# A hybrid SSD and MLA layer on one core: TensorE's issue order up to the first FFN tiles is replaced by another

## The chip, the core and the metric

The kernel runs on one core of a Trainium2 chip. The metric is the device time of one execution in microseconds. Three runs of the kernel before gave 641.02, 641.30 and 641.71 us, a median of 641.3 us. One further execution was profiled.

## What is computed

One layer of a streaming encoder in float32, for 512 new tokens of one stream and 64 tokens of another that has a cache of 256. SSD heads and latent attention heads run side by side on one projection; a SwiGLU FFN follows.

```python
h = rmsnorm(x, p['norm_mix'])
proj = h @ p['w_in']                       # z, x/B/C, dt, query latent, key/value latent
xbc, conv_new = causal_conv(xbc, conv_buf, p['conv_w'], p['conv_b'])
y, h_new = ssd_scan(xh, dt, A, Bm, Cm, ssm_h0)
y = y + d_skip * xh
y_ssd = rmsnorm(y * silu(z), p['ssd_norm'])
...
o_lat = mla_attend(q_lat, q_rope, q_pos, keys_c, keys_r, jnp.arange(P + T))
o = einsum('bthl,lhd->bthd', o_lat, w_uv)
x = x + concatenate([y_ssd, o], -1) @ p['w_out']
hf = rmsnorm(x, p['norm_ffn'])
x = x + (silu(hf @ p['w_gate']) * (hf @ p['w_up'])) @ p['w_down']
```

The model is 1024 wide, the FFN 2816; there are 8 SSD heads of 64 channels with 128 states, and 8 attention heads of 64. Outputs are the final norm of x, the new latents, the SSD states and the last convolution rows.

## The kernel before

All 576 tokens lie along the free dimension and channels along the 128 partitions. TensorE (PE) works with two kinds of products.

- Weight products are split in two float32r parts each and summed over three products: `product` (L120 to L130, the input projection), `product_halves` (L435 to L446, the gate z, the query and key tiles ps_q and ps_k, the output projection ps_o), `v_tiles` (ps_v, L590) and `block_product` (L852, the FFN). A tile of tokens is 288 columns, half of 576.
- Products of data with data stay float32, and each is recorded as two passes: the SSD's ps_y, ps_i and ps_s (L527, L538, L548), the sums ps_g (L572), the scores sc and sc_s (L657, L663), and the values pv and pvs (L704, L715). Transposes through the identity (ps_x, ps_b, ptp; L483, L491, L679, L687) are float32 too, with one pass each.

Some of the float32 products use only half of PE's columns. ps_y has 64 channels for each head: the even head writes partitions 0 to 63 and the odd head 64 to 127, as two products of 64 columns that stand one behind the other in the program. sc_s (the scores of the 64 late tokens), pv and pvs are built in the same way. The profile shows the columns in the shape: `128*64` or `100*64` or `64*64` where the others read `128*128`. With one exception (ps_v of the 64-token block) the float32r products are 128 columns wide.

In the order of the program: eight steps that load x and the first weights (ps_first), the twelve tiles of the input projection with convolution (ps_in, then ps_z), five SSD chunks (`chunk_a`, `chunk_e`, `chunk_b`, `chunk_s`, `gate`, numbered 4, 0, 1, 2, 3; chunk 4 is the 64-token stream), four pairs of attention heads (`scores`, `soft`, `turn`, `values`), the output projection, and the FFN. The FFN's first tile is ps_p (`gu_first`); from the second on the tiles are called ps_x, ps_y and ps_z again, and the down projection ps_d.

PSUM holds three buffers called sc, three pp and two hm. VectorE (DVE) takes the row maximum of each score tile (mx, L640), ScalarE (ACT) the exponential (pr, L641), which is the last reader of an sc buffer. The reader of ps_y on DVE is L532.

Each engine's order is written out by hand in the table `ISSUE`, by numbers of the instructions in the order in which the code makes them. `issue_in_order` at the end of the kernel ties each instruction to the one ahead of it, so an engine executes in exactly that order, and every engine waits in its place for what it needs:

```python
order = list(_places(text))
for a, b in zip(order, order[1:]):
    tc.add_manual_dep(made[b], made[a].name, info, reason="issue order")
```

Of the kernel before, what the change touches and what calls it, by code (L numbers as in the profile page):

```python
# [1295 lines left out]
def issue_in_order(tc, nc):  # L1296
# [10 lines left out]

ISSUE = {
    "PE": """
0-7 20-21 8 14-16 9-13 22-25 38-41 17-19 32-36 26-31 42-43 56-59 37 50-55 68-69 44-47 60-61 74-79 92 48-49 62-67 80-85  # L1310
98-99 93-97 70-73 86-91 104-106 100-103 110 107-109 122-126 134-135 111-115 128-133 148-153 116-121 136-141 127
142-147 154-169 174-175 170-171 270-274 176-221 172-173 222-269 275-370 373-420 371 421-468 372 469-634 637 641-644
638-640 657-660 635-636 665-697 661 698-718 662 737-758 719-720 663-664 721-726 763 645-652 759-760 727-736 764-766
653-656 767-768 771-794 769-770 795-818 859 761-762 819-826 860-861 833-836 862-864 837-840 827-832 865-870 841-845
871-872 846-852 873-874 853-856 875-877 880 878-879 857-858 881-887 904-911 888 912 892-899 889-891 900-903 925-926
913-921 927-935 922-924 939-940 936-938 949-957 964-966 941 945-948 967 958-963 968-969 942-944 970-975 987 976-979
1003 980-986 991-993 988 1004-1005 1015-1021 1006-1014 1022-1024 994-996 1025-1026 1029-1034 1043-1045 997-998 989
1000-1002 999 1046-1054 990 1035-1039 1059-1061 1040-1042 1062-1064 1027-1028 1075-1077 1081-1092 1055-1056 1078-1080
1057 1093-1096 1058 1097-1104 1121-1123 1071-1072 1124-1129 1065 1068-1070 1073 1105-1107 1066-1067 1074 1130-1143
1119 1144-1156 1120 1229-1232 1157 1108-1112 1233-1240 1113-1114 1158 1241-1245 1115-1118 1159-1161 1246-1247 1176  # L1320
1253-1262 1177 1248-1252 1263-1264 1162-1175 1180 1178 1181-1182 1265 1183 1266-1268 1277-1278 1179 1279 1184-1187
1190-1195 1269-1275 1196-1204 1188-1189 1205-1223 1276 1227-1228 1224-1226 1280-1297 1301-1303 1298-1300 1304-1321
1342-1343 1348-1355 1344-1347 1322-1341 1356-1511 1572 1512-1559 1575-1576 1560-1571 1577 1596-1598 1578 1573-1574
1593 1584-1585 1579 1581-1583 1602-1604 1623-1625 1594-1595 1614 1586 1605-1606 1590-1592 1611-1613 1632-1634
1587-1589 1608-1610 1607 1580 1599-1601 1620-1622 1641 1626-1628 1647-1648 1629-1631 1649 1642-1643 1615-1616
1635-1637 1617-1619 1638-1640 1653 1656 1658-1667 1644-1646 1650-1652 1654-1655 1668-1669 1657 1682 1694-1705
1683-1693 1670-1681 1730-1741 1706-1729 1742-1748 1754-1755 1749-1753 1756-1767 1778-1785 1768-1777 1786-1885
1898-1905 1886-1897 1906-2017 2030-2036 2018-2029 2037-2053 2066-2084 2054-2065 2085-2089 2102-2104 2090-2101
2105-2221 2234-2236 2240-2241 2222-2233 2237 2242-2248 2238-2239 2249-2725 2738-2740 2744 2726-2737 2741 2745-2751
2742-2743 2752-3229 3242-3244 3248 3230-3241 3245 3249-3255 3246-3247 3256-3733 3746-3748 3752 3734-3745 3749  # L1330
3753-3759 3750-3751 3760-4189
""",
    "DVE": """
1 0 2-3 48 4-5 7 6 9 12 8 10-11 13-15 17 16 18-20 23 21-22 49 24 58 25 30 26 85 27-29 31-34 67-68 106 36 69 108 37 105
# [161 lines left out]
```

## Time and profile before

| what | value |
|---|---|
| median of three runs | 641.3 us |
| the profiled execution's own time | 639.76 us |
| its span, first to last instruction | 638.1 us |
| mean granted PE clock | 0.998 |
| PE busy | 627.0 us (98%), 4635 matmul records |
| DVE busy | 543.5 us (85%) |
| ACT busy | 400.9 us (63%) |

A record's start is measured, its end is modelled, and products overlap: a float32r product of 288 columns is listed with some 0.295 us, but the next one starts earlier than that. So the work of PE is read here from one start to the next. In a timeline row the first number is the start, the second the time to the end of the last record of the row, then come the engine, the line, the operation, its output and inputs, the shape and the number of records. A float32 product counts as two records, a transpose as one.

### The profile page before, as it was taken

The numbers are of one execution on the slowest core, as the hardware profiler recorded it, in microseconds if no ns is written. First come the engines' busy times: TensorE is split into PE (matmuls) and PEld (weight loads), VectorE is DVE, ScalarE is ACT, GpSimd is POOL, SyncE is SP. The second block draws the span as 40 slices with busy tenths as digits, with TensorE's granted clock in tenths as the row PEclk, the third lists the DMA queues.
The fourth block names the chain that finished last, engine by engine and source line by source line (L and its number), as shares of the span: only waits on it lengthen the run. The fifth ranks groups of instructions, "written<-read, shape, count | busy, mean of one in ns | idle before, by whom it ended". The sixth has DMA issues, their size and how long they took to land.

```text
span 638.1 us, 12090 instructions
## 1 busy us (share of the span) xinstructions
PE 627.0 (98%) x4635; PEld 598.9 (94%) x4635; DVE 543.5 (85%) x945; ACT 400.9 (63%) x768; POOL 110.4 (17%) x164
## 2 busy tenths in 40 slices
PE   9999999999999999999999999999999999999996
PEld 8899999986787799999999999999999999999995
DVE  6999986899876699999999888988899789986555
ACT  7645436778775567766566676566757665767364
POOL 1322103101010000001300330033103220323323
PEclk9999999999999999999999999999999999999999
DMA  9322366322231133235643986398737892589914
GB/s 320 130 61 71 97 158 159 108 80 60 87 123 61 56 111 102 89 116 183 239 141 101 205 185 153 82 186 194 169 100 156 197 206 100 101 211 258 259 27 148
DMA packets 39593, 89.19 MB, mean 140 GB/s; under 512 B 4570, under 2 KB 14312, under 8 KB 39280
## 3 DMA queue, kind: packets, MB, share of 16 engines
q1 hardware_dynamic: 26416, 63.12, 30.5%
q0 software_dynamic: 12400, 24.73, 20.9%
q8 instruction: 36, 0.59, 0.4%
q10 hardware_dynamic: 720, 0.57, 0.3%
q14 instruction: 21, 0.17, 0.1%
HBM read 62.74 MB, written 24.53 MB: 137 GB/s over the span
## 4 chain that ended last, share of the span: by engine, by line
PE 84%; DVE 3%; ACT 1%; issue 1%; POOL 1%; DMA 1%; POOLq 0%; DVEq 0%; ACTq 0%
PE ps_x L852 21%; PE ps_d L1050 14%; PE ps_z L852 11%; PE ps_o L443 8%; PE ps_y L852 5%; PE ps_in L128 4%; PE ps_z L443 3%; PE ps_l L988 3%; PE ps_d L988 2%; PE ps_p L852 2%; PE sc L657 2%; PE pv L704 2%; PE ptp L679 1%; PE ps_v L590 1%; PE ps_q L443 1%
## 5 line engine op out<-in xcount | busy, mean ns | idle before, releaser
L852 PE MATMUL ps_x<-xop,wh_gu_S 128*128 128x288 f32 x504 | 101.7, 295 | 0.0
L852 PEld LDWEIGHTS ps_x<-xop,wh_gu_S 128*128 128x128 f32 x504 | 80.7, 188 | 0.2
L852 PE MATMUL ps_x<-xop,wl_gu_S 128*128 128x288 f32 x252 | 74.0, 294 | 0.0
L113 DVE TENSOR_TENSOR wl_gu_S<-gu,wh_gu_S 128x1024 fp32r<-128x1024 f32 x44 | 53.4, 1221 | 10.3 <-ACT wh_gu_S L112 6.8
L1064 POOL DMA_DIRECT2D acc<-fz x32 | 27.9, 907 | 167.2 <-ACT fz L1061 138.3
L112 ACT CAST wh_gu_S<-gu 128x1024 fp32r<-128x1024 f32 x44 | 46.3, 1052 | 15.9 <-PE ps_y L852 8.2
L852 PEld LDWEIGHTS ps_x<-xop,wl_gu_S 128*128 128x128 f32 x252 | 47.3, 188 | 0.0
L128 PE MATMUL ps_in<-xs,wh_in 128*128 128x288 f32 x256 | 45.3, 298 | 0.8 <-DVE sp_a L351 0.6
L128 PEld LDWEIGHTS ps_in<-xs,wh_in 128*128 128x128 f32 x256 | 37.6, 189 | 1.9 <-issue 0.9
L852 PE MATMUL ps_z<-xop,gu_a 128*128 128x288 f32 x252 | 38.3, 295 | 0.0
L852 PEld LDWEIGHTS ps_z<-xop,gu_a 128*128 128x128 f32 x252 | 35.0, 188 | 0.0
L852 PE MATMUL ps_z<-xop,wh_gu_S 128*128 128x288 f32 x168 | 34.9, 297 | 0.0
L852 PE MATMUL ps_x<-xop,wh_gu_A 128*128 128x288 f32 x168 | 34.6, 297 | 0.0
L852 PE MATMUL ps_y<-xop,wh_gu_A 128*128 128x288 f32 x168 | 33.9, 294 | 0.0
L112 ACT CAST wh_gu_A<-gu 128x1024 fp32r<-128x1024 f32 x22 | 23.1, 1051 | 10.4 <-PE ps_x L852 7.0
L443 PE MATMUL ps_o<-cat_y,wh_out 128*128 128x288 f32 x128 | 29.3, 312 | 0.4 <-ACT cat_y L142 0.4
L113 DVE TENSOR_TENSOR wl_gu_A<-gu,wh_gu_A 128x1024 fp32r<-128x1024 f32 x22 | 26.8, 1220 | 1.4 <-ACT wh_gu_A L112 1.0
L852 PEld LDWEIGHTS ps_z<-xop,wh_gu_S 128*128 128x128 f32 x168 | 27.2, 189 | 0.3 <-ACT wh_gu_S L112 0.3
L128 PE MATMUL ps_in<-xs,wl_in 128*128 128x288 f32 x128 | 27.4, 296 | 0.0
L852 PEld LDWEIGHTS ps_x<-xop,wh_gu_A 128*128 128x128 f32 x168 | 27.2, 189 | 0.1
L852 PEld LDWEIGHTS ps_y<-xop,wh_gu_A 128*128 128x128 f32 x168 | 26.9, 188 | 0.0
L443 PE MATMUL ps_z<-xs,wh_z 128*128 128x288 f32 x128 | 26.4, 299 | 0.0
(384 smaller groups left out, 2012.0 us busy)
## 6 DMA issues: line engine op xcount, KB each, us to landing
gu<-in_w_gu SPq DMA_DIRECT2D x44, 512.0 KB, 5.3
wr_d<-in_w_down SPq DMA_DIRECT2D x18, 512.0 KB, 4.1
acc<-fz POOLq DMA_DIRECT2D x16, 288.0 KB, 6.6
acc<-da POOLq DMA_DIRECT2D x16, 288.0 KB, 7.8
acc<-dc POOLq DMA_DIRECT2D x16, 288.0 KB, 8.4
wr_in<-in_w_in SPq DMA_DIRECT2D x8, 512.0 KB, 3.8
wr_out<-in_w_out SPq DMA_DIRECT2D x8, 512.0 KB, 3.2
cumb<-cumD SPq DMA_DIRECT2D x5, 512.0 KB, 4.6
```

What stands on the lines that cost most here:

```text
L112: act.copy(hi, raw)
L113: dve.tensor_tensor(lo, raw, hi.bitcast(F32), ALU.subtract)
L128: pe.matmul(ps[:m, hf, :n], w, x[:, hf * n : (hf + 1) * n], start=start and k == 0 and i == 0, stop=stop and k == last and i == 2,)
L443: pe.matmul(ps[:, :n], w, x[:, cols], start=k == 0 and i == 0, stop=k == len(terms) - 1 and i == 2,)
L590: pe.matmul(ps[:n], l, r, start=j == 0, stop=j == 2)
L657: pe.matmul(s[:, :nk], qs[:, j, q0 : q0 + P], ks[:, j, :nk], start=True, stop=True)
L679: pe.transpose(pp[:, k : k + P], prs[p, i][:, j, b * P : b * P + P], ident)
L704: pe.matmul(pv[64 * j : 64 * j + 64, b * P :], V[b][:, h * HD : (h + 1) * HD], pts[p, b, j], start=b == 0, stop=True, skip_group_check=b > 0,)
L852: pe.matmul(ps, p, q, start=not onto and first and kp == kps[0] and j == 0, stop=onto or (last and kp == kps[-1] and j == 2), skip_group_c ...
L988: pe.matmul(ps, w, x[:, cols], start=first and k == 0 and i == 0, stop=last and k == len(terms) - 1 and i == 2,)
L1050: pe.matmul(ps, p, v, start=not onto and n == 0 and j == 0, stop=onto or (n == len(ks) - 1 and j == 2), skip_group_check=onto,)
L1064: pool.dma_start(out, src, accum_op=ALU.add)
```

## The change

Only PE's row of the table `ISSUE` is replaced. The instructions are the same, 4396 products, and DVE, ACT, POOL and SP keep every place. Up to number 1755 places are exchanged, from there on the order is the same. Two lines of the table before and two of it now:

```diff
-1057 1093-1096 1058 1097-1104 1121-1123 1071-1072 1124-1129 1065 1068-1070 1073 1105-1107 1066-1067 1074 1130-1143
-1119 1144-1156 1120 1229-1232 1157 1108-1112 1233-1240 1113-1114 1158 1241-1245 1115-1118 1159-1161 1246-1247 1176
...
+1093-1097 1058 1098-1104 1121-1123 1071 1124-1129 1065 1068-1070 1105-1106 1072 1066 1073 1107 1067 1074 1130-1156
+1119-1120 1229-1247 1253-1254 1248-1250 1255-1260 1251-1252 1261-1264 1157-1158 1108-1115 1176 1116-1118 1159-1161
```

Counted through the whole order, stretches of one data type (float32r or float32) go from 113 to 73. Stretches of one width of the array (the products' rows and columns) go from 48 to 76.

Three places show what moves. All are on PE. The last number is the output's partitions and columns: 64 partitions mean a product of 64 columns. The order lists each product once.

The first place is the end of the SSD: ps_y of chunk 3 (ps_y_1846), its state products ps_i_1859 and ps_s_1866, and the key tiles of the first two pairs. Before:

```order
L527 MATMUL ps_y_1846<-E_1739,xdt_1727 64x128 x8
L538 MATMUL ps_i_1859<-bc,h_1843 128x128
L443 MATMUL ps_k_1_1834<-ckv,wh_pair_1825 128x416 x2
L443 MATMUL ps_k_1_1834<-ckv,wl_pair_1826 128x416
L548 MATMUL ps_s_1866<-xw_1749,bt_1734 128x256 x2
L538 MATMUL ps_i_1859<-bc,h_1843 128x128 x3
L443 MATMUL ps_k_0_1891<-ckv,wh_pair_1825 128x416 x2
```

Now:

```order
L443 MATMUL ps_k_1_1834<-ckv,wh_pair_1825 128x416 x2
L443 MATMUL ps_k_1_1834<-ckv,wl_pair_1826 128x416
L527 MATMUL ps_y_1846<-E_1739,xdt_1727 64x128 x4
L538 MATMUL ps_i_1859<-bc,h_1843 128x128
L527 MATMUL ps_y_1846<-E_1739,xdt_1727 64x128 x2
L548 MATMUL ps_s_1866<-xw_1749,bt_1734 128x256 x2
L527 MATMUL ps_y_1846<-E_1739,xdt_1727 64x128 x2
L538 MATMUL ps_i_1859<-bc,h_1843 128x128 x3
L443 MATMUL ps_k_0_1891<-ckv,wh_pair_1825 128x416 x2
```

The key tile ps_k_1_1834 now stands ahead of ps_y, and the eight products of ps_y stand in three pieces with ps_i and ps_s between them; the last two are behind ps_s.

The second place is pair 2 of the attention: the scores sc_s of the late tokens, between the key tile and the query tile of pair 3, and transposes of pair 1 (ptp_1). Before:

```order
L443 MATMUL ps_k_0_2368<-ckv,wl_pair_2245 128x416
L663 MATMUL sc_s<-ks_383,qs_382 64x320 x2
L443 MATMUL ps_q_1_2374<-cqn_481,wh_pair_2244 128x288 x2
L443 MATMUL ps_q_1_2374<-cqn_481,wl_pair_2245 128x288
L443 MATMUL ps_q_1_2374<-cqn_484,wh_pair_2244 128x288 x2
L443 MATMUL ps_q_1_2374<-cqn_484,wl_pair_2245 128x288
L679 MATMUL ptp_1_0_2253<-ident,pr_1_2079 128x128
L679 MATMUL ptp_1_1_2258<-ident,pr_1_2079 128x128
```

Now:

```order
L663 MATMUL sc_s<-ks_383,qs_382 64x320
L443 MATMUL ps_q_1_2374<-cqn_481,wh_pair_2244 128x288 x2
L443 MATMUL ps_q_1_2374<-cqn_481,wl_pair_2245 128x288
L443 MATMUL ps_q_1_2374<-cqn_484,wh_pair_2244 128x288 x2
L443 MATMUL ps_q_1_2374<-cqn_484,wl_pair_2245 128x288
L679 MATMUL ptp_1_0_2253<-ident,pr_1_2079 128x128
L679 MATMUL ptp_1_1_2258<-ident,pr_1_2079 128x128
L679 MATMUL ptp_1_1_2258<-ident,pr_2_2065 128x128
L679 MATMUL ptp_1_1_2258<-ident,pr_3_2023 128x128
L679 MATMUL ptp_2_0_2331<-ident,pr_2_2065 128x128
L679 MATMUL ptp_2_0_2331<-ident,pr_3_2023 128x128
L663 MATMUL sc_s<-ks_383,qs_382 64x320
```

The two products of sc_s stood side by side; now the second one follows twelve products later, among transposes.

The third place is the end of pair 2 and the scores of pair 3: sc_s of pair 3, the values pv and pvs of pair 2, and transposes of both. Before:

```order
L657 MATMUL sc_0_0_2500<-ks_385,qs_384 128x128
L657 MATMUL sc_0_1_2502<-ks_385,qs_384 128x128
L663 MATMUL sc_s<-ks_385,qs_384 64x320 x2
L704 MATMUL pv_2553<-pt_0_2487,V_1659 64x512 x2
L704 MATMUL pv_2553<-pt_1_2521,V_1659 64x384 x2
L704 MATMUL pv_2553<-pt_2_2532,V_1670 64x256 x2
L704 MATMUL pv_2553<-pt_2_2532,V_1670 64x128 x2
L715 MATMUL pvs_2565<-pts_2514,V_1681 64x64 x4
L715 MATMUL pvs_2565<-pts_2514,V_1692 64x64 x2
L679 MATMUL ptp_2_0_2575<-ident,pr_2_2479 128x128
```

Now:

```order
L663 MATMUL sc_s<-ks_385,qs_384 64x320
L679 MATMUL ptp_2_1_2538<-ident,pr_2_2279 128x128
L679 MATMUL ptp_2_1_2538<-ident,pr_3_2211 128x128
L663 MATMUL sc_s<-ks_385,qs_384 64x320
L679 MATMUL ptp_2_1_2538<-ident,pr_3_2211 128x128
L704 MATMUL pv_2553<-pt_0_2487,V_1659 64x512 x2
L704 MATMUL pv_2553<-pt_1_2521,V_1659 64x384 x2
L657 MATMUL sc_1_0_2585<-ks_385,qs_384 128x256
L704 MATMUL pv_2553<-pt_2_2532,V_1670 64x256 x2
L704 MATMUL pv_2553<-pt_2_2532,V_1670 64x128 x2
L715 MATMUL pvs_2565<-pts_2514,V_1681 64x64
L679 MATMUL ptp_2_0_2575<-ident,pr_2_2479 128x128
```

The two products of sc_s are apart, a score product stands inside pv, and three transposes stand behind the first product of pvs, whose other five follow.

In the same way ps_y of chunk 4 is cut in two, ps_y of chunk 0 in three (its first two products stand alone), ps_y of chunk 1, which ps_v of the 64-token block cut behind the first product, is cut behind the third by ps_i, one score product stands between pv of pair 0 and sc_s of pair 1 (the products pvs among pv now stand together), and three float32r products each stand inside the transposes of ps_dt and of chunk 4. On the other side, ps_z, ps_o and the transposes stand together in longer stretches: the transposes of chunk 0 (ps_b_1314), for instance, stood at three places among ps_z and now stand with those of chunk 1.

More of the change, by code (lines that the diff above doesn't have):

```diff
@@ L1309 @@
     "PE": """
[L1310 to L1318, printed above, removed]
-1057 1093-1096 1058 1097-1104 1121-1123 1071-1072 1124-1129 1065 1068-1070 1073 1105-1107 1066-1067 1074 1130-1143
@@ L1320 @@
-1119 1144-1156 1120 1229-1232 1157 1108-1112 1233-1240 1113-1114 1158 1241-1245 1115-1118 1159-1161 1246-1247 1176
[L1321 to L1329, printed above, removed]
@@ L1330 @@
-2742-2743 2752-3229 3242-3244 3248 3230-3241 3245 3249-3255 3246-3247 3256-3733 3746-3748 3752 3734-3745 3749
-3753-3759 3750-3751 3760-4189
+0-7 20-21 8 14-16 9-13 22-24 17 25 18-19 38-39 32-33 40-41 34-36 26-31 44 37 45 42-43 56-59 50-55 68 60 69 61 74 46-49
+62-66 70-72 75 67 80-85 98 76-79 92 73 86 93-96 87-88 99-103 89-91 104-108 116-118 109 122 119 97 123 134-135 124-125
+120-121 126 110-115 128-133 148-153 127 136-147 154-171 270-271 174-176 272-274 177-225 172-173 226-269 275-370
+373-419 421-429 420 371 430-447 469-472 448 473-475 449-460 372 461-468 476-512 517-532 513-516 533-591 613-615
@@ new lines @@
+592-596 616-620 597 621 598-602 622-624 603-610 625-633 611-612 637-638 634-636 641-644 639-640 657-660 665-721
+737-760 722-736 661-663 763-766 664 645-650 767-768 653-654 651-652 655-656 771-775 795-799 776-777 800 778 801-802
+779-787 803-807 788-794 808-818 761-762 819 769 820 770 833-835 821-826 836-840 859-864 827 831-832 828-830 865-868
+841-843 880-883 869-873 845-847 853-854 848-852 844 855-856 874-879 857-858 884-887 904-912 888-903 913-915 925-926
+916-924 927-930 935 931-932 939-940 933-934 936-938 949-957 964-966 941 945-948 967-968 958-963 969 942-944 970-974
@@ new lines @@
+976-982 975 987 983-986 991-993 988 1003-1004 1015 1005-1007 1016-1019 1008-1014 1020-1026 1029-1034 1043-1045 994-999
+989 1046 1049-1054 1047-1048 1000-1002 1035-1041 1059-1064 1042 990 1027-1028 1075-1076 1081-1092 1055-1057 1077-1080
+1093-1097 1058 1098-1104 1121-1123 1071 1124-1129 1065 1068-1070 1105-1106 1072 1066 1073 1107 1067 1074 1130-1156
+1119-1120 1229-1247 1253-1254 1248-1250 1255-1260 1251-1252 1261-1264 1157-1158 1108-1115 1176 1116-1118 1159-1161
+1177 1162-1175 1178 1265-1268 1277-1279 1179-1180 1188 1181-1187 1190-1192 1269-1273 1193-1197 1189 1198-1201 1205
@@ new lines @@
+1202-1203 1206 1204 1207-1210 1227 1211-1215 1221-1223 1216-1220 1274 1280 1275-1276 1228 1224-1226 1281-1286 1289
+1287-1288 1290-1322 1342-1343 1348-1355 1344-1347 1323-1341 1356-1449 1452-1453 1450-1451 1454-1511 1575 1512-1523
+1572-1573 1578 1524-1547 1579 1548-1559 1580 1560-1561 1599 1562-1571 1581-1583 1590-1592 1611-1612 1574 1584-1586
+1605 1600-1602 1587-1589 1603 1608-1609 1593-1594 1610 1606 1595 1629-1630 1613 1620-1621 1614-1616 1576-1577 1635
+1604 1623-1625 1636-1637 1607 1631 1626 1632 1596-1597 1622 1641-1643 1598 1617 1627-1628 1647 1618-1619 1638-1640
@@ new lines @@
+1633-1634 1648 1656 1649 1644 1653 1658-1665 1645-1646 1650 1666-1668 1651 1669 1657 1654-1655 1682 1694-1702 1652
+1703-1705 1683-1693 1670-1681 1730-1741 1706-1729 1742-1748 1754-1755 1749-1753 1756-1767 1778-1785 1768-1777
+1786-1885 1898-1905 1886-1897 1906-2017 2030-2036 2018-2029 2037-2053 2066-2084 2054-2065 2085-2089 2102-2104
+2090-2101 2105-2221 2234-2236 2240-2241 2222-2233 2237 2242-2248 2238-2239 2249-2725 2738-2740 2744 2726-2737 2741
+2745-2751 2742-2743 2752-3229 3242-3244 3248 3230-3241 3245 3249-3255 3246-3247 3256-3733 3746-3748 3752 3734-3745
@@ L1332 @@
+3749 3753-3759 3750-3751 3760-4189
 """,
```

## Prediction

> **What bounds the kernel now.** The page comes first: the span, the busy times and the chain of work that ended last.
>
> ```profile
> span 638.1 us, 12090 instructions
> PE 627.0 (98%) x4635; PEld 598.9 (94%) x4635; DVE 543.5 (85%) x945; ACT 400.9 (63%) x768; POOL 110.4 (17%) x164
> PE 84%; DVE 3%; ACT 1%; issue 1%; POOL 1%; DMA 1%; POOLq 0%; DVEq 0%; ACTq 0%
> ```
>
> PE is busy for 98% of the span and holds 84% of the chain. The windows by stage show whether it has room anywhere. Their columns are the stretch, its length, then for PE, PEld, DVE, ACT and POOL the busy time with the number of records, PE's clock, the DMA share and GB/s.
>
> ```profile
> 94.00:147.00 53.00, 52.20 (x408) 47.27 (x408) 44.81 (x86) 35.74 (x91) 9.26 (x13) 1.00 0.42 110
> 147.00:163.00 16.00, 14.12 (x69) 8.82 (x67) 15.71 (x39) 15.24 (x44) 1.95 (x4) 1.00 0.43 143
> 163.00:222.00 59.00, 58.97 (x428) 47.36 (x428) 40.85 (x101) 37.30 (x105) 1.91 (x4) 1.00 0.17 60
> 222.00:270.00 48.00, 48.00 (x356) 47.23 (x356) 46.44 (x85) 33.50 (x54) 0.00 (x0) 1.00 0.30 101
> 270.00:400.00 130.00, 130.00 (x980) 129.79 (x979) 121.03 (x185) 82.58 (x140) 22.59 (x32) 1.00 0.60 167
> 400.00:620.00 220.00, 220.00 (x1653) 220.00 (x1652) 183.41 (x277) 138.24 (x242) 49.34 (x55) 1.00 0.70 161
> ```
>
> From 163 us to 620 us PE has no gap, so whatever PE starts later at 163 us, or does more slowly behind it, should reach the end whole. The one stretch with room is 147 to 163 us, the start of the attention: 1.88 us without PE work, with DVE busy for 15.71 of 16. The list of PE's waits names what it waits for there; the columns behind the colon are total, times and longest, in us.
>
> ```profile
> PE sc L657 <- ACT pr L641: 1.1, 2, 0.9
> PE ps_x L483 <- DVE qt L422: 0.8, 1, 0.8
> PE sc_s L663 <- ACT pr L641: 0.2, 1, 0.2
> ```
>
> The scores wait 1.1 us for an exponential to free their buffer, and exponentials follow the maxima that DVE takes. So the start of the attention goes by DVE.
>
> **Unit costs.** The last window gives a float32r product of 288 columns: 220.00 / 1653 = 0.133 us from start to start, so 0.192 for 416 columns and 0.236 for 512. The timeline gives a float32 pass:
>
> ```profile
> 216.77 1.36 PE L679 MATMUL ptp<-ident,pr 128*128 128x128 f32 x11
> 217.97 0.49 PE L687 MATMUL ptp_s<-ident,pr 128*64 128x128 f32 x3
> 218.22 0.51 PE L443 MATMUL ps_o<-cat_y,wh_out 128*128 128x288 f32 x2
> 218.56 0.29 PE L443 MATMUL ps_o<-cat_y,wl_out 128*128 128x288 f32 x1
> ```
>
> From 216.77 to 218.56 stand 14 transposes and two products of 0.133: (1.79 - 0.27) / 14 = 0.109 us for a pass of 128 columns. Three of the transposes are only 64 wide, at no price that shows.
>
> **What it removes: changes of data type, 113 stretches to 73.** One such place, with a transpose among gate products:
>
> ```profile
> 101.92 0.29 PE L443 MATMUL ps_z<-xs,wl_z 128*128 128x288 f32 x1
> 102.05 0.27 PE L491 MATMUL ps_b<-ident,bc 128*128 128x128 f32 x1
> 102.08 0.52 PE L443 MATMUL ps_z<-xs,wh_z 128*128 128x288 f32 x2
> 102.43 0.30 PE L443 MATMUL ps_z<-xs,wl_z 128*128 128x288 f32 x1
> 102.57 0.43 PE L443 MATMUL ps_z<-xs,wh_z 128*128 128x288 f32 x2
> 102.83 0.29 PE L443 MATMUL ps_z<-xs,wl_z 128*128 128x288 f32 x1
> ```
>
> From 101.92 to 102.83 are 0.91 us. Six products at 0.133 and one transpose at 0.109 make 0.907. The two products behind the transpose take 0.35 instead of 0.27, but the transpose itself only 0.03. I take **0.00 us** for 40 fewer changes. The bounds: 0.085 a change if that late start (0.35 - 0.27) counted in full, 40 x 0.085 = 3.4 us gained, and 0.0 on the other side, since nothing here becomes dearer when such changes go.
>
> **What it adds: changes of the array's width, 48 stretches to 76.** The price of a visit to 64-column products shows at ps_y of chunk 3 and at sc_s of pair 2:
>
> ```profile
> 142.20 0.29 PE L443 MATMUL ps_q<-cqn,wl_pair 128*128 128x288 f32 x1
> 142.43 1.09 PE L527 MATMUL ps_y<-E,xdt 128*64 128x128 f32 x16
> 143.45 0.49 PE L538 MATMUL ps_i<-bc,h 128*128 128x128 f32 x2
> 143.69 0.63 PE L443 MATMUL ps_k<-ckv,wh_pair 128*128 128x416 f32 x2
> 144.16 0.35 PE L443 MATMUL ps_k<-ckv,wl_pair 128*128 128x416 f32 x1
> ...
> 181.52 0.35 PE L443 MATMUL ps_k<-ckv,wl_pair 128*128 128x416 f32 x1
> 181.80 0.76 PE L663 MATMUL sc_s<-ks,qs 100*64 100x320 f32 x4
> 182.49 0.54 PE L443 MATMUL ps_q<-cqn,wh_pair 128*128 128x288 f32 x2
> 182.86 0.29 PE L443 MATMUL ps_q<-cqn,wl_pair 128*128 128x288 f32 x1
> ```
>
> Sixteen records of ps_y take 142.43 to 143.45: side by side, the even and the odd head run as one, 8 passes x 0.109 = 0.87, where 16 would be 1.74. The work from 142.20 to 144.16 is 0.133 + 0.87 + 2 x 0.109 + 2 x 0.192 = 1.61; measured 1.96, so **0.35 for a visit** of two changes. For sc_s: 0.192 + 2 x 2.5 x 0.109 (two passes of 320 columns, both halves at once) + 2 x 0.133 = 1.00; measured 1.34, so 0.34. Here too four records run in the time of two, so an sc_s product that stands alone costs a full 0.545 more for the pair. A third place has three changes in a row:
>
> ```profile
> 120.21 0.39 PE L590 MATMUL ps_v<-wh_uv,ckv 128*128 128x512 f32 x1
> 120.53 1.13 PE L548 MATMUL ps_s<-xw,bt 64*128 64x256 f32 x4
> 121.59 1.09 PE L527 MATMUL ps_y<-E,xdt 128*64 128x128 f32 x16
> 122.62 0.51 PE L590 MATMUL ps_v<-wl_uv,ckv 128*128 128x512 f32 x1
> 122.96 0.39 PE L590 MATMUL ps_v<-wh_uv,ckv 128*128 128x512 f32 x1
> ```
>
> Work 0.236 + 4 x 2 x 0.109 + 0.87 + 0.236 = 2.21, measured 2.75: 0.54, or 0.18 a change. From ps_s to ps_y both are float32 and only the shape changes, yet 1.06 us (120.53 to 121.59) stand for 0.87 of work; so it is the width that costs, not the data type.
>
> A rule speaks against this change in so many words. The Trainium skill, page "TensorEngine Tiling (Array Packing)", section "Key Properties", says that a change of the tiling mode, unlike one of the tile, drains TensorE; the 0.35 us for a visit agree. It gives no figure; 28 more changes at the 0.175 of the rows above would be 4.9 us by that rule, were every change to cost the same, which the narrow transposes above deny.
>
> **The sum up to the attention.** ps_y of chunk 4 in two pieces: one visit more, 0.35 (bounds 0 and 0.35). ps_y of chunk 0 in three: two visits, 0.70, and the first two products no longer side by side, 2 x 0.109 = 0.22; together 0.92 (bounds 0.22, if a change next to a transpose is free, and 0.92). ps_y of chunk 1 had one cut already, by products of its own width, and now gets a wide one: 0.2, between 0 and 0.35. The three float32r products within ps_dt and within chunk 4's transposes: taken as 0, bounds 0 and two visits, 0.70; they lie ahead of the waits for DVE (qt, above), which cover what they cost. So far 1.47.
>
> Then ps_y of chunk 3, the first place shown. Its last product now has ahead of it the key tile ps_k_1 (3 x 0.192 = 0.58), one ps_i (0.22), two products ps_s of 256 columns (4 x 2 x 0.109 = 0.87) and two visits more (0.70): it is 2.37 us later, on top of the 1.47. Who waits for it shows on DVE:
>
> ```profile
> 143.58 0.46 DVE L607 COPY qs<-ps_q 64x288 f32<-64x288 f32 x1
> 144.07 0.61 DVE L532 SCALAR_TENSOR_TENSOR xsd<-xsd,par,ps_y 128x128 f32<-128x128 f32 x2
> 148.96 1.66 DVE L640 TENSOR_REDUCE mx<-sc 128x1 f32<-128x512 f32 x3
> ```
>
> All heads of the chunk are one PSUM tile, and the first L532 waits for the last of its products. Before, ps_y is done at 142.43 + 1.09 = 143.52, and DVE comes to it at 144.07: 0.55 of slack. So DVE is held for 2.37 - 0.55 = 1.82, with L532, the state updates and then the first row maxima queued behind it, for which ACT's exponentials and PE's scores wait. Bounds: 0, if the waits of the stretch take it all, and 2.37. I take 1.82, since DVE's 15.71 of 16 us there leave it no room to catch up. PE's own two visits (0.70) lie within that wait and are not counted again. At 163 us the kernel is **1.47 + 1.82 = 3.29 us** late.
>
> **The sum behind 163 us**, where PE has no gap. pv of pair 0: pvs stands together, a wide score product comes between pv and sc_s: one visit less what is saved, 0.2 (0 to 0.35). sc_s of pair 2 (second place): the halves apart, 0.545, and one visit, 0.34: 0.89. sc_s of pair 3 (third place): apart, 0.545; pvs' first product without its neighbour, two passes of 64 columns, 2 x 0.055 = 0.11; and sc_s, pv and pvs, one visit before, are now cut at four points (by two transposes, by one, by a score product within pv, by three transposes), 4 x 0.35 = 1.4. That is 2.05; the lower bound leaves only the score product as a visit, 0.545 + 0.11 + 0.35 = 1.0. Sum 0.2 + 0.89 + 2.05 = **3.14**; bounds 0.545 + 1.0 = 1.55 and 3.3.
>
> Together 3.29 + 3.14 = **+6.4 us**. The profiled execution took 639.76 (1.66 around its span of 638.1), 1.5 below the median of 641.3. Its span would become 644.5, its time 646.2, and the median **647.7**. With the upper bound of the gain by data types, 3.4, it would be 644.3.
>
> **Rivals.** (1) *The waits at the attention's start absorb the first half.* PE has 1.88 us there; if ps_y's lateness doesn't hold DVE, PE's own additions (1.47 + 0.70 = 2.17) shrink to 0.3, and with 3.14 behind it the time is 644.7. Against it: those waits are for engines that themselves follow PE's products. (2) *Faster: the 0.35 of a visit is the price of its two changes of data type, 0.175 each, and not of the width.* The place is every border between ps_z, ps_o and float32 products. Then the new visits, most of them among float32 products, cost nothing; what is left is the broken pairs, 0.22 + 0.545 + 0.545 + 0.11 = 1.42, and ps_y's wait without visits, 2.37 - 0.70 - 0.55 = 1.12, together +2.5. Against that stand 40 borders less: it decides from 2.5 / 40 = 0.063 us a border, and at 0.175 the kernel gains 7.0 - 2.5 = 4.5, to 636.8. Against it: the row at 101.92, where a border costs 0.00, and that of ps_s and ps_y, where no type changes. (3) *Further waits*: sc_s and transposes of pairs 2 and 3 are later, and DVE and ACT need them. PE has no wait behind 163 us now, so no row has a price; I take 1.5, between 0 and the 1.82 of ps_y and nearer to it, since a late sc_s holds the same chain over DVE and ACT: 649.2. (4) *A change of width is as free as in the narrow transposes*: the +2.5 of rival 2 without its gain, 643.8. Against it: the 0.35 at three places. That the change doesn't do what it says is excluded for the data types by the count, 113 to 73; the rows decide only what that is worth.
>
> **How the numbers follow.** Forecast 0.58, rival 1 0.15, rival 3 0.10, rival 4 0.07: 0.90, all slower. Rival 2 has 0.10: 0.04 for a price a border well above 0.063 (faster), 0.06 for one about it (same, within 0.2%, which is 1.3 us and about what a measurement of this kernel can tell from no change). The range is to hold 8 in 10: it begins at 643.4, just below rival 4, and ends at 649.8, rival 3 with the 0.55 of slack in ps_y's wait gone too. Left out are 0.10 of rival 2 and some 0.08 at the ends.
>
> **What would show it.** A first L532 of chunk 3 that waits some 1.8 us for PE, with ps_y's records in three rows; ps_z and ps_o at 0.133 from start to start, no faster where transposes no longer stand among them; sc_s as two separate rows of 0.55 or more; the work of 163 to 222 us in 62 instead of 59; the FFN of the same length as before. I am wrong if DVE does not wait for ps_y, if the single sc_s rows take 0.27, or if the gate and output projection stretches become shorter than the count of their products times 0.133.

## The result, and the profile after

The kernel after took a median of 648.15 us (645.7 to 648.9, six runs), the one before 641.16 us in six runs beside it: a ratio of 1.0102, with a 95% interval of 1.0085 to 1.0119. The forecast was 647.7 us, in a range from 643.4 to 649.8. The size was right, in part by luck: a price was missing and other terms came out too high, as the profile shows.

The profiled execution took 648.47 us. The page after, the same three lines as before:

```profile
span 646.8 us, 12091 instructions
PE 634.9 (98%) x4635; PEld 601.5 (93%) x4635; DVE 542.6 (84%) x945; ACT 399.9 (62%) x768; POOL 113.1 (17%) x164
PE 82%; DVE 4%; ACT 2%; issue 1%; POOL 1%; POOLq 0%; DVEq 0%; ACTq 0%
```

The span is 8.7 us longer and PE is busy for 7.9 us more, with the same 4635 records. The windows, three long ones and then the stretch around the start of the attention in short ones (PEclk is the third number from the right):

```profile
147.00:163.00 16.00, 13.27 (x70) 8.82 (x67) 15.51 (x40) 12.52 (x37) 1.95 (x4) 0.98 0.22 69
163.00:222.00 59.00, 59.00 (x369) 43.52 (x369) 38.20 (x93) 36.34 (x99) 1.92 (x4) 0.95 0.21 71
400.00:620.00 220.00, 220.00 (x1653) 220.00 (x1653) 185.48 (x277) 135.55 (x231) 46.58 (x52) 1.00 0.72 167
155.00:163.00 8.00, 6.14 (x32) 3.65 (x31) 7.83 (x25) 7.75 (x26) 1.95 (x4) 0.95 0.35 106
163.00:170.00 7.00, 7.00 (x23) 4.61 (x23) 5.70 (x11) 3.92 (x8) 0.00 (x0) 0.57 0.48 175
170.00:180.00 10.00, 10.00 (x76) 7.96 (x75) 6.74 (x15) 7.43 (x18) 0.00 (x0) 1.00 0.00 0
```

In the FFN nothing moved: 1653 records in 220 us, as before. Between 163 and 170 us stands a number that no such row of before has: a granted clock of 0.57. The trace's clock records give half the clock from 162.2 us on, for 6.83 us.

Since the products are the same in both kernels, the starts of the same product can be compared, wherever the sets of products ahead of it are the same too. The difference (after less before, in us) grows like this; behind it stands what the prediction had summed up to there:

| up to | measured | predicted |
|---|---|---|
| ps_z, ahead of the first stretch around chunk 4 (88.8 us before) | +0.55 | 0 |
| behind chunk 4's transposes (97.7) | -0.40 | 0 |
| behind ps_y of chunk 4 (113.4) | -0.06 | +0.35 |
| behind ps_y of chunk 0 (125.0) | +0.74 | +1.27 |
| query tile ahead of ps_y of chunk 3 (141.4) | +1.24 | +1.47 |
| ps_g behind the held DVE (149.8) | +3.12 | +3.29 |
| sc1_3_0, the last score product ahead of the moved transposes (156.7) | +3.12 | +3.29 |
| ps_o behind them (163.0) | +6.05 | +3.29 |
| behind pv of pair 0 and sc_s of pair 1 (174.9) | +6.17 | +3.5 |
| behind sc_s of pair 2 (184.9) | +7.00 | +4.4 |
| behind pair 3's scores and pv (213.8) | +8.63 | +6.4 |
| end | +8.70 | +6.4 |

The profiled execution of before was a quick one: 639.76 us, 1.4 below its median, while that of after lies 0.3 above its own. Hence +8.7 between the traces and +7.0 between the medians.

**The end of the SSD.** PE's timeline of after, ps_y of chunk 3 in its three pieces:

```profile
143.99 0.34 PE L443 MATMUL ps_k<-ckv,wl_pair 128*128 128x416 f32 x1
144.26 0.66 PE L527 MATMUL ps_y<-E,xdt 128*64 128x128 f32 x8
144.85 0.49 PE L538 MATMUL ps_i<-bc,h 128*128 128x128 f32 x2
145.27 0.44 PE L527 MATMUL ps_y<-E,xdt 128*64 128x128 f32 x4
145.64 1.13 PE L548 MATMUL ps_s<-xw,bt 128*128 128x256 f32 x4
146.70 0.44 PE L527 MATMUL ps_y<-E,xdt 128*64 128x128 f32 x4
```

Each border costs again: eight records take 0.59 us for 0.44 of work, the two of ps_i 0.42 for 0.22, the four of ps_s 1.06 for 0.87. The last product ends at 147.14. DVE's timeline has the other side of it; the bracket gives the idle time ahead and what ended it:

```profile
144.72 0.46 DVE L607 COPY qs<-ps_q 64x288 f32<-64x288 f32 x1
147.19 0.61 DVE L532 SCALAR_TENSOR_TENSOR xsd<-xsd,par,ps_y 128x128 f32<-128x128 f32 x2 [2.01 <-PE ps_y L527]
152.08 1.61 DVE L640 TENSOR_REDUCE mx<-sc 128x1 f32<-128x512 f32 x3
```

DVE waits 2.01 us for the last piece, and the first row maximum starts at 152.08 instead of 148.96, 3.12 later.

**The start of the attention.** PE's waits there, and its timeline:

```profile
PE sc L657 <- ACT pr L641: 0.9, 1, 0.9
PE ps_g L572 <- ACT ysq L569: 0.8, 1, 0.8
PE ptp L679 <- DVE pr L647: 0.6, 1, 0.6
```

```profile
159.85 1.12 PE L657 MATMUL sc<-ks,qs 100*128 100x512 f32 x2 [0.92 <-ACT pr L641]
161.61 1.70 PE L679 MATMUL ptp<-ident,pr 128*128 128x128 f32 x7 [0.64 <-DVE pr L647]
163.11 3.19 PE L657 MATMUL sc<-ks,qs 100*128 100x512 f32 x4
166.10 0.42 PE L679 MATMUL ptp<-ident,pr 128*128 128x128 f32 x1
```

The wait of ps_g is new: here PE meets the held DVE, for ps_g needs the squares ysq, which ACT takes of DVE's late xsd. The score products behind it wait as long as before. The wait of the transposes is new too: seven of them now stand ahead of the score products sc1_3_1 and sc1_2_0 instead of behind them, need pr from DVE and are at PE's head too early. In return two waits of the order before are gone, 0.21 us of a score product and 0.39 of ps_o, together about as much as the new one:

```profile
158.92 0.91 PE L657 MATMUL sc<-ks,qs 100*128 100x384 f32 x2 [0.21 <-ACT pr L641]
160.66 0.40 PE L443 MATMUL ps_o<-cat_y,wh_out 128*128 128x288 f32 x1 [0.39 <-ACT cat_y L142]
```

The half clock shows in the four score records behind the transposes (512 and 384 columns, two passes each, 14 x 0.109 = 1.53 us): they take 2.99 us. The seven transposes take 1.50 us for 0.76 of work, but little of that is the clock's: in experiment 6 the same seven take 1.40 us at the full clock (b8), and the score records 1.51.

**The late products.** A score pair side by side took 0.69 us from start to start before (181.80 to 182.49). After:

```profile
190.30 0.75 PE L663 MATMUL sc_s<-ks,qs 100*64 100x320 f32 x2
190.99 0.33 PE L679 MATMUL ptp<-ident,pr 128*128 128x128 f32 x1
...
214.65 0.75 PE L663 MATMUL sc_s<-ks,qs 100*64 100x320 f32 x2
215.33 0.44 PE L679 MATMUL ptp<-ident,pr 128*128 128x128 f32 x2
215.70 0.75 PE L663 MATMUL sc_s<-ks,qs 100*64 100x320 f32 x2
216.38 0.33 PE L679 MATMUL ptp<-ident,pr 128*128 128x128 f32 x1
```

One half alone takes 0.69 (190.30 to 190.99) and 0.68, as long as the two took together.

### The profile page after: what moved, and what is told of

It reads as the page before. It is cut to its first block, busy times and chain, and to the rows that moved or that the text cites. A ratio compares the mean times of both kernels' runs of the same rounds, so it can differ in the third digit from the quotient of the medians.

```text
span 646.8 us, 12091 instructions
## 1 busy us (share of the span) xinstructions
PE 634.9 (98%) x4635; PEld 601.5 (93%) x4635; DVE 542.6 (84%) x945; ACT 399.9 (62%) x768; POOL 113.1 (17%) x164
## 4 chain that ended last, share of the span: by engine, by line
PE 82%; DVE 4%; ACT 2%; issue 1%; POOL 1%; POOLq 0%; DVEq 0%; ACTq 0%
PE ps_x L852 20%; PE ps_d L1050 14%; PE ps_z L852 10%; PE ps_o L443 7%; PE ps_y L852 5%; PE ps_in L128 4%; PE ps_z L443 4%; PE ps_l L988 3%; PE sc L657 2%; PE ps_d L988 2%; PE ptp L679 2%; PE pv L704 1%; DVE xop L800 1%; PE ps_y L527 1%; PE ps_q L443 1%
## 5 line engine op out<-in xcount | busy, mean ns | idle before, releaser
L443 PE MATMUL ps_o<-cat_y,wh_out 128*128 128x288 f32 x128 | 27.3, 307 | 0.0
L1050 PE MATMUL ps_d<-pair,d_1h 128*128 128x288 f32 x128 | 26.2, 294 | 0.0
```

What stands on the lines that cost most here:

```text
L443: pe.matmul(ps[:, :n], w, x[:, cols], start=k == 0 and i == 0, stop=k == len(terms) - 1 and i == 2,)
L1050: pe.matmul(ps, p, v, start=not onto and n == 0 and j == 0, stop=onto or (n == len(ks) - 1 and j == 2), skip_group_check=onto,)
```

## The experiments

All are made of the two orders: a label beginning with a starts from the changed order, one with b from the order before. Rows are PE's. Ratios are to the kernel before, run on the same chip beside them.

**1. The stretch around ps_y of chunk 3, taken back and put in alone.** The edit to the changed order (a1); in b1 the same stretch goes the other way into the order before:

```diff
-ps_k_1_1834 x3
-ps_y_1846 x4
-ps_i_1859
-ps_y_1846 x2
+ps_y_1846 x8
+ps_i_1859
+ps_k_1_1834 x3
 ps_s_1866 x2
-ps_y_1846 x2
 ps_i_1859 x3
```

> The changed order, with the one stretch around ps_y of chunk 3 as before (14 products; ps_y in one piece, ahead of ps_i, the key tile and ps_s). Theory: the late last product of ps_y holds DVE for 2.0 us (its first L532 in the changed kernel's trace), and the half clock of 6.8 us at the start of the attention follows from the longer wait there. Then this gives back 2.0 us with the full clock and about 4 without the half clock: 644 to 646 us, and L532 waits less than 0.3 us. Rival: the waits at the start of the attention take ps_y's lateness up and only PE's own two visits count: 647.4 us or more.

> The order before, with that one stretch as in the changed kernel (51 stretches of one width instead of 48). Theory: DVE held 1.8 to 2.0 us, time 643.2 us with a full clock and some 645 where the half clock comes with it. Rival (absorbed by the waits): at most the two visits, 641.9 us. That a longer wait alone brings the half clock: it shows in this kernel's trace or its granted clock is below 0.997; if the clock stays full, the wait of ps_y isn't enough for it.

Measured: a1 645.0 us (ratio 1.0072, 1.006 to 1.0084), 3.15 less than the changed kernel, or 2.7 when each is taken against the kernel before beside it. b1 644.99 us (1.0062, 1.0046 to 1.0078). DVE's timeline in a1 and then in b1:

```profile
145.10 0.46 DVE L607 COPY qs<-ps_q 64x288 f32<-64x288 f32 x1
145.59 0.61 DVE L532 SCALAR_TENSOR_TENSOR xsd<-xsd,par,ps_y 128x128 f32<-128x128 f32 x2
```

```profile
148.35 0.60 DVE L532 SCALAR_TENSOR_TENSOR xsd<-xsd,par,ps_y 128x128 f32<-128x128 f32 x2 [2.36 <-PE ps_y L527]
```

With ps_y whole L532 doesn't wait; with ps_y cut it waits 2.36 us, in the order before too. In b1's trace the starts are 2.05 later behind the stretch (from +2.23 to +4.28). The absorbing waits (rival 1) are refuted: 642.48 is b1's fastest run, above their 641.9. But a1 keeps the half clock:

```profile
159.00:166.00 7.00, 6.46 (x20) 4.02 (x19) 7.00 (x15) 6.20 (x14) 0.71 (x2) 0.52 0.77 261
```

So the half clock doesn't need ps_y's lateness; this part of the expectation is wrong. Nor does the lateness bring it each time: in b1's trace the clock is full up to the end of the kernel. b1's median, at +4.25, is about twice the 2.05 of its trace; none of its six runs has a granted clock of 0.998 or more, but where the others lose the rest isn't shown.

**2. The long stretches of one data type without the cuts.** All 64-column pieces of the changed order are joined again:

```diff
-ps_y_1846 x4, ps_i_1859, ps_y_1846 x2, ps_s_1866 x2, ps_y_1846 x2
+ps_y_1846 x8, ps_i_1859, ps_s_1866 x2
...
-sc_s, ptp_2_1_2538 x2, sc_s, ptp_2_1_2538
+ptp_2_1_2538 x3, sc_s x2
-pv_2553 x4, sc_1_0_2585, pv_2553 x4, pvs_2565, ptp_2_0_2575 x3, pvs_2565 x5
+pv_2553 x8, pvs_2565 x6, sc_1_0_2585, ptp_2_0_2575 x3
```

> The changed order with every cut piece of 64-column products joined again (ps_dt, chunk 4's transposes, ps_y of chunks 4, 0, 1 and 3, pv of pair 0, sc_s of pairs 2 and 3, pv and pvs of pair 2); the longer stretches of one data type stay: width changes 75 to 48, data type changes 69 to 67 (before: 47 and 109). Theory (width costs, data type costs nothing): the time of before less what the better cover of chunk 4's transposes saves (up to 0.8 us of a wait), 640.4 to 641.4 us, clock full. Rival (a price of 0.063 to 0.175 us for a change of data type): 40 of them less, 634 to 638.7 us.

Measured: 639.81 us, ratio 0.999 (0.9977 to 1.0002). 40 changes of data type fewer than before are worth nothing that shows, and rival 2 is refuted. The 8.3 us between this kernel and the changed one come with the cuts and what follows from them. The full clock of the expectation did not come: the trace has half the clock for 3.41 us at the start of the attention, and the median lies 0.6 us below the expected range all the same.

**3. More changes of data type.** The counter-test, in the order before:

```diff
-ptp_1_1_2104 x4
-ps_k_1 x3, ps_q_1 ...
+ptp_1_1_2104, ps_k_1, ptp_1_1_2104, ps_k_1, ptp_1_1_2104, ps_k_1, ptp_1_0_2099, ps_q_1 ...
```

> The order before with 44 more changes of data type and none of width: eight stretches of three to five full-width transposes are interleaved one by one with the float32r products behind them (data type changes 109 to 153). Theory (a change of data type costs nothing): 640.7 us, within 0.5. Rival (0.063 to 0.175 us each): 2.8 to 7.7 us more, 643.5 to 648.4 us; at the 0.085 of the late start behind a transpose 3.7 us more.

Measured: 641.52 us, ratio 1.0007 (0.9998 to 1.0017), -0.1 to +1.1 us for 44 changes, at most 0.025 each; the median is 0.8 above the expected 640.7, of which 0.15 is the kernel before beside it. By matched starts the trace shows 0.4 us over the interleaved stretches, 0.01 each. The timeline of b3:

```profile
169.90 0.47 PE L443 MATMUL ps_k<-ckv,wh_pair 128*128 128x416 f32 x1
170.20 0.27 PE L679 MATMUL ptp<-ident,pr 128*128 128x128 f32 x1
170.23 0.43 PE L443 MATMUL ps_k<-ckv,wh_pair 128*128 128x416 f32 x1
170.50 0.27 PE L679 MATMUL ptp<-ident,pr 128*128 128x128 f32 x1
170.52 0.44 PE L443 MATMUL ps_k<-ckv,wl_pair 128*128 128x416 f32 x1
```

A transpose shows 0.02 to 0.03 us to the next start and a product of 416 columns 0.27 to 0.30; two of each, from 169.90 to 170.52, take 0.62, and their work is 2 x (0.192 + 0.109) = 0.602.

**4. Cuts alone.** In the order before, pv of pair 1 is cut between its pairs, pv of pair 3 inside one:

```diff
-ps_o_4_1, ps_o_5_0 x2
-pv_2438 x8
+pv_2438 x2, ps_o_4_1, pv_2438 x2, ps_o_5_0, pv_2438 x2, ps_o_5_0, pv_2438 x2
...
-ps_o_6_0, pvs_2754 x2, pv_2764 x8
+pvs_2754 x2, pv_2764, ps_o_6_0, pv_2764 x7
```

> The order before with pv of pair 1 cut three times between its pairs of halves by one float32r product each (three more visits, no pair broken), and pv of pair 3 cut once inside its first pair of 512 columns (one visit, one broken pair). Theory: 3 x 0.35 = 1.05 us in pv of pair 1, and 0.35 + 0.87 (2 passes x 512 columns at 0.109 for 128) = 1.22 us in pv of pair 3, together 2.3 us, 643.0 us. Rival (a change of width free): 0.87 us, all of it in pair 3, 641.6 us. Rival (a single half costs nothing): 1.4 us, 642.1 us.

Measured: 642.92 us, ratio 1.0033 (1.0021 to 1.0046), +2.1 us. PE's timeline at both places:

```profile
199.60 1.08 PE L704 MATMUL pv<-pt,V 128*64 128x512 f32 x4
200.61 0.40 PE L443 MATMUL ps_o<-cat_y,wl_out 128*128 128x288 f32 x1
200.94 0.87 PE L704 MATMUL pv<-pt,V 128*64 128x384 f32 x4
201.74 0.40 PE L443 MATMUL ps_o<-cat_y,wh_out 128*128 128x288 f32 x1
202.07 0.65 PE L704 MATMUL pv<-pt,V 128*64 128x256 f32 x4
202.65 0.40 PE L443 MATMUL ps_o<-cat_y,wl_out 128*128 128x288 f32 x1
202.98 0.44 PE L704 MATMUL pv<-pt,V 128*64 128x128 f32 x4
203.35 0.71 PE L715 MATMUL pvs<-pts,V 64*64 64x64 f32 x12
...
221.23 1.07 PE L704 MATMUL pv<-pt,V 128*64 128x512 f32 x2
222.23 0.40 PE L443 MATMUL ps_o<-cat_y,wh_out 128*128 128x288 f32 x1
```

From 199.60 to 203.35 are 3.75 us; the work is 2 x 10 x 0.109 + 3 x 0.133 = 2.58, so 1.17 for three visits, 0.39 each. One half of 512 columns alone takes 1.00 (221.23 to 222.23), as the pair does (1.01 at 199.60). By matched starts pair 1 costs 1.1 and pair 3 1.2 us more than before. Width and broken pairs both cost, at the sizes expected.

**5. The late cuts alone**, in the order before: the second and third place of the change, and pv of pair 0.

```diff
-sc_s x2, ps_q_1 x6, ptp x4
+sc_s, ps_q_1 x6, ptp x6, sc_s
...
-sc_s x2, pv_2553 x8, pvs_2565 x6
+sc_s, ptp x2, sc_s, ptp, pv_2553 x4, sc_1_0_2585, pv_2553 x4, pvs_2565, ptp x3, pvs_2565 x5
```

> The order before, with only three later stretches as in the changed kernel: pv of pair 0 with a score product behind it, sc_s of pair 2 apart, sc_s, pv and pvs of pair 3 and 2 cut. Theory (visits of 0.35 and broken pairs): 2.5 us more (between 2.1 and 3.1), 643.7 us, full clock, no new wait of PE. Rival (a change of width free, only broken pairs count): 0.545 + 0.545 + 0.11 = 1.2 us more, 642.4 us.

Measured: 644.37 us, ratio 1.006 (1.0046 to 1.0074), +3.6, above the 2.1 to 3.1 expected; by matched starts 3.1 us from the first of the three stretches to the end, 2.9 of it up to the end of the third. The full clock failed here too, though not through the late cuts: in this trace PE loses its clock at chunk 4's transposes, where the order is that of before, behind a wait of 1.9 us for DVE's qt.

```profile
97.20:100.60 3.40, 3.40 (x17) 2.79 (x16) 3.40 (x6) 1.16 (x2) 2.50 (x6) 0.50 0.98 201
```

Rival 4 (1.2 us) is refuted: the fastest run, 643.38, lies above its 642.4.

**6. The start of the attention.** Two stretches, taken back in the changed order (a4) and in the joined one (a3), put alone into the order before (b6), and then one by one (b7, b8). The second stretch moves the score product sc1_2_0 and the product ps_o_0_0 as well as sc1_3_1:

```diff
-sc0_2_0
 ps_q_1_1912 x6
+sc0_2_0
...
-ptp0_0_0 x4, ptp0_0_1 x3
 sc1_3_1, sc1_2_0
+ptp0_0_0 x4, ps_o_0_0, ptp0_0_1 x3
 ptp0_0_1
```

> The changed order with only those two stretches at the start of the attention as before; ps_y of chunk 3 stays in three pieces. Theory: the wait of 0.6 us for DVE's pr at the transposes goes, and the half clock of 3.4 to 6.8 us comes less often or shorter: 1 to 2 us less than the changed kernel, 646 to 647 us. Rival (the half clock follows from ps_y's lateness alone): 0.6 us less at most, 647.5 us, clock 0.992 in most runs.

> The joined order of the second last experiment's kind (changed order, 64-column products joined) with two short stretches at the start of the attention as before: the score product sc1_3_1 ahead of the transposes of pair 0 instead of behind seven of them, and the query tile ps_q_1 ahead of sc0_2_0. Theory: in the joined kernel's trace PE waits 0.6 us for DVE's pr at those transposes, right behind a wait of 0.9 us, and a half clock of 3.4 us follows; without that wait the two are apart and the half clock comes less often: 638.3 to 639.3 us, granted clock more often 0.999. Rival: the half clock and the wait are not tied to these two stretches: same as joined, 639.8 us, clock 0.996 as there.

> The order before with only the two stretches at the start of the attention as in the changed kernel (sc1_3_1 behind seven transposes of pair 0; sc0_2_0 ahead of the query tile). Nothing of width changes (47 changes). Theory: PE waits 0.6 us more at the transposes for DVE's pr, and the half clock falls there in most runs: 641.5 to 643 us, granted clock 0.997 or less in most runs. Rival: the half clock needs ps_y's lateness too: 640.8 us, clock 0.999 in most runs.

> The order before with one of the two stretches alone: the score product sc0_2_0 ahead of the six products of the query tile ps_q_1 instead of behind them. Theory: the half clock comes with the transposes ahead of sc1_3_1, so this stretch changes nothing: 640.9 us, granted clock 0.998 or more in about half of the runs, as before. Rival: it comes with this stretch: 642.2 us, no run at 0.998 or more.

> The order before with the other stretch alone: sc1_3_1 behind seven transposes of pair 0. Theory: the half clock comes with it: 642.2 us, no run or hardly one at a granted clock of 0.998 or more. Rival: it changes nothing, 640.9 us, clock 0.998 or more in about half of the runs.

| kernel | transposes ahead of sc1_3_1 | median us | ratio, interval | runs with a clock of 0.998 or more |
|---|---|---|---|---|
| before (beside all of these) | no | 640.6 to 641.2 | 1 | 43 of 86 |
| b7 | no | 640.78 | 1.0006, 0.9994 to 1.0018 | 7 of 11 |
| b8 | yes | 641.8 | 1.0016, 1.0002 to 1.0029 | 0 of 12 |
| b6 | yes | 642.28 | 1.0016, 1.0004 to 1.0027 | 0 of 12 |
| a4 | no | 646.51 | 1.0082, 1.0068 to 1.0097 | 1 of 4 |
| changed kernel | yes | 648.15 | 1.0102, 1.0085 to 1.0119 | 0 of 6 |
| a3 | no | 639.2 | 0.9966, 0.9953 to 0.9979 | 3 of 6 |
| a2 | yes | 639.81 | 0.999, 0.9977 to 1.0002 | 0 of 12 |

The window of 163 to 170 us in a4, where the changed kernel has a clock of 0.57:

```profile
163.00:170.00 7.00, 6.48 (x42) 5.13 (x41) 6.98 (x13) 4.20 (x9) 0.00 (x0) 1.00 0.55 204
```

The lower clock goes with the stretch of the transposes: with a1, 47 runs of five kernels have them ahead of sc1_3_1, and none of them reaches 0.998; the query tile alone (b7) changes nothing. Alone the stretch costs 1.0 us by its ratio (b8); taken out of the changed order together with the query tile (a4) it gives 1.6 us between the medians, 1.3 when each is taken against the kernel before beside it, and the two intervals still overlap. A run's mean clock doesn't say where the clock was lost, though. Every trace also has half the clock over the last 1.1 to 7.2 us of its span, and a run at 0.997 can have it there alone, as the profiled ones of a3, a4, b1 and b8 do. Behind the moved transposes, or just ahead of them, the half clock stands in four of the five traces with that order; b8's has none. There the new wait for pr shows without it:

```profile
157.94 1.12 PE L657 MATMUL sc<-ks,qs 100*128 100x512 f32 x2 [0.91 <-ACT pr L641]
159.70 1.56 PE L679 MATMUL ptp<-ident,pr 128*128 128x128 f32 x7 [0.64 <-DVE pr L647]
161.10 1.68 PE L657 MATMUL sc<-ks,qs 100*128 100x512 f32 x4
162.61 0.27 PE L679 MATMUL ptp<-ident,pr 128*128 128x128 f32 x1
```

And the wait costs nothing on balance: in b8's trace PE is 1.21 us behind that of before ahead of the moved products and 1.20 behind them, since the two waits of before are gone. In b6's trace the half clock begins at 158.1, ahead of the transposes (159.43), which then have no wait; in a1's it begins at 159.2, with the transposes at 160.10. In b4's, which up to there has the order of before, it begins at 157.7. So a half clock at this place doesn't need that wait, nor the moved transposes. That the stretch makes it more frequent is what the runs show (b8 against b7); how it does so stays open.

a3, the joined order with the start of the attention as before, is the fastest kernel of all: 639.2 us, 0.3% below the kernel before. It too has 40 changes of data type fewer, so its gain of about 2 us is a point for rival 2. Its trace answers it: by matched starts it gains 1.05 us on before at chunk 4's transposes, where a wait goes (experiment 7), and only 0.26 from there to 278 us, less than 0.01 a change.

**7. Where the gain at chunk 4's transposes comes from.** In the order before, the ps_z products around them as in the joined order:

```diff
-ps_x_1249, ps_b_1256 x4, ps_x_1249 x3, ps_x_1307 x4
-ps_z_1_1214 x2
+ps_z_1_1214 x2
+ps_x_1249 x2, ps_b_1256 x4, ps_x_1249 x2, ps_x_1307 x4
```

> The order before with one stretch of 57 products ahead of and around chunk 4's transposes in the joined form of the changed order: the last products of ps_z stand ahead of the first ps_x instead of two of them behind it, and the two tiles of ps_z are interleaved. Theory: the wait of ps_x for DVE's qt (0.8 to 1.9 us in every trace with the order before, none with the changed one) goes in part or whole: 639.6 to 640.3 us, that wait below 0.5 us. Rival: the wait has its cause elsewhere (what DVE does before qt) and stays: 640.8 us.

Measured: 640.55 us, ratio 0.9991 (0.9981 to 1.0001), and the wait is still there, 1.1 us. The theory fails. In the eight traces with the order before at this place ps_x waits 0.8 to 1.9 us for DVE's qt; in the five of the changed order it doesn't. Ahead of qt in DVE's queue stands the split of a weight of the gate, which waits for ACT and so for the load wr_z; four of these loads landed 3.7 to 8.3 us after their issue in the trace of before, 4.1 to 5.6 in that of after, and 4.2 to 8.6 in b5's. Which part of the earlier order saves the wait, and how much of it is chance, stays open.

## Why the prediction was right, and where not

- **A change of data type costs nothing: right.** The price of 0.00 from the row at 101.92 holds: 44 more cost at most 1.1 us (b3), 0.4 in the trace; 40 fewer gain at most 1.5 (a2 against before), and of the 2 us that a3 gains its trace leaves 0.26 to them.
- **A visit to 64-column products costs 0.35, a broken pair its full time: right.** b4 measured 0.39 and 1.2 us where 0.35 and 1.22 were expected. The rule of the Trainium skill that a change of tiling mode drains TensorE (page "TensorEngine Tiling (Array Packing)", section "Key Properties") agrees.
- **ps_y of chunk 3 holds DVE: right.** 2.01 us of wait for 1.82; b1 shows it alone. DVE doesn't catch up, as the prediction said: the first maximum is 3.12 later. The way back to PE is another than the one named, though: not the maxima, exponentials and scores pass the delay on first, but ACT's squares ysq to ps_g, which waits 0.76 us. PE's own two visits lie within the hold, as the sum had it: from +1.24 to +3.12 are 1.88.
- **Up to the attention, 3.29: right in the sum, not in all its terms.** 3.12 was measured up to 156.7 us. "They lie ahead of the waits for DVE (qt, above), which cover what they cost" took that wait as lasting; it went, -0.95 at this place. Against that stand the 0.55 by which this execution was late ahead of chunk 4, and 0.50 instead of 0.2 between 125.0 and 141.4 us. That these nearly cancel is luck.
- **At 163 us, 3.29: wrong.** 6.05 was measured. The sum stopped at DVE's wait. The transposes set ahead of sc1_3_1 were not priced at all, though the order shows them moved; their wait costs nothing on balance (b8), the half clock does.
- **PE's clock: not in the prediction.** In the profiled execution the table goes from +3.12 to +6.05 over the start of the attention, where a4's trace, with a full clock, goes from +3.72 to +3.88. So some 2.8 us of that execution are a term that the prediction lacked. In the median it is 1.3 to 1.6, by two intervals that overlap.
- **The late cuts, 3.14: a little high.** 2.65 in the changed kernel's trace and 2.8 to 3.1 in b2's. sc_s of pair 2 came out at 0.83 to 0.89 for 0.89, the third place at 1.6 to 1.7 for 2.05, pv of pair 0 at 0.1 to 0.3 for 0.2.
- **The total: near by luck in part.** a4 has all that the sum priced and not the moved transposes: its median is 5.7 us above the one of before beside it, where the sum gave 6.4. The changed kernel, with them, has 7.0. So the sum was somewhat high for what it priced, and the term that it lacked made up for it.
- **Rival 1** (absorbed waits) falls by b1, **rival 2** by a2 and b3, **rival 4** by b4 and b2. **Rival 3** (further waits) named waits for the late sc_s and transposes of pairs 2 and 3; none shows in the trace. The new waits, of ps_g and of pair 0's transposes, stand ahead of there.

## What to carry to other kernels

When the order of one engine is searched by a count, price that count first: here a transpose among weight products at full width was free, and each cut of half-width products cost 0.35 us plus the broken pair. Keep early the last product of a group that another engine's queue waits for: here the last 0.2 us of ps_y, put behind other work, held DVE for 2 us. And where PE's waits gather, read its granted clock as well as their length: in six of fourteen traces half the clock followed such a place.

## What had not been expected of the hardware

Within the kernels the half clock came in periods of 3.41 and 6.83 us, and the full clock ahead of it had lasted 27, 45 or 46 times 3.413 us in the six traces that show one, so PE's clock is decided on a fixed grid. The Trainium skill says so too: page "TensorE: Matmul & The Clock Gate", section "What's actually happening", gives a free-running window of 3413 ns. It has the clock halved behind a window of idleness; here PE was idle for only 1.15 to 1.89 us of the 3.41 in the window ahead of a half clock, and up to 1.60 us in other windows within the kernel that had none behind them. Idle time alone is therefore not the criterion, and what is remains open. In the kernel before, runs with a granted clock of 0.998 or more have a median of 640.5 us, those below 0.994 of 641.8: its spread goes with the clock. Three places for a half clock show in traces with this order: the start of the attention (b4), chunk 4's transposes (b2) and the end of the kernel (all). How often each of them counts isn't shown.
